# A hybrid decoder layer: loads of the opening in order of use over two queues, and row factors turned on chip before they are stored

## The chip, the cores and the metric

The kernel runs on one core of a Trainium2 chip. The metric is the device time of one execution in microseconds (us). Five engines work beside each other: PE (TensorE, matmuls; its weight loads are PEld), DVE (VectorE), ACT (ScalarE), POOL (GpSimd) and SP (SyncE, which here only issues transfers). Each engine takes its instructions in a fixed order and waits on semaphores. SP, ACT and POOL can issue DMA transfers; sixteen DMA engines carry them out.

## The reference

One inference step of one layer for 4096 prompt tokens and 64 sample tokens (8 sequences of 8), 1024 features each, in float32:

```python
h = x * rsqrt(mean(x * x, axis=-1) + eps) * g_pre      # one factor per token, one gain per feature
z = h @ w_in                                           # 1024 -> 2816 columns, split into
cb, cc, ch, cg, q, k, v, ag, mq, mg = split(z)         # conv, attention and memory groups
u = cc * ch;  conv = conv_w[0]*u[t-2] + conv_w[1]*u[t-1] + conv_w[2]*u[t]
out_a = silu(cg) * cb * conv                           # new conv state: the last two rows of u
out_b = silu(ag) * window_attention(q, k, v, sink)     # 128-wide causal window, one sink per head
out_c = silu(mg) * memory_attention(mq, mk, mv)        # 256 memory tokens
y = concat(out_a, out_b, out_c) @ w_out
x = x + rmsnorm(y) * g_post
```

Outputs are the new x for prompt and sample tokens, the new window keys and values, the convolution's states (two rows of u per sequence; called o_convp for the prompt and o_convs for the eight sample sequences) and the memory's keys and values.

## The kernel before

The 4160 tokens stand as columns, 520 to a block, eight blocks (b = 0 to 7), each of two halves of HW = 260. The in-projection is done in three phases of the weight's columns, 0, 1 and 2, all eight blocks in each. Within a block the product of a 2x2 split of weights (A11, A12, A21, A22) and of inputs (B11 to B22) is made with seven products over sums and differences of the parts (S1 to S4, T1 to T3). Only blocks 0 and 1 of phase 0 are "plain", with eight products of the parts themselves. The name of a buffer tells the part: x_0B is a part B of block 0, w_0A a part A of weight quarter 0, lo_2T the low half of a T of block 2, place a buffer that keeps an input part of a block.

float32 is kept by splitting each operand into hi (a rounded copy) and lo (the rest); `product` (L392) makes hi·hi, lo·hi and hi·lo over four k of 128 features, twelve matmuls of 128x128 by 128x260 to a bank; a product has four banks in phases 0 and 1, thus 48 matmuls, and is called a step here. DVE adds the banks into z (`evict`, L399). In phase 2 the attention runs between the products, and the output projection (L1675) follows.

The order of all engines' work is written out: in each step a list of jobs is put between the matmuls, and each engine's instructions stand in the order in which the program writes them.

**Opening.** SP and ACT issue the loads of the first input part x(0, B11) (in two halves of k, 128x2x260 each, written x_0B) and of the four quarters of the weight part A21 (wr_0A to wr_3A), then of A11. While they fly PE runs idle matmuls (L737). DVE copies w_0A's hi part, ACT makes hi_0B (x times the gain, L613), DVE lo_0B and w_0A's lo part; then the 48 matmuls of the first product begin. In this first step each bank takes hi·hi for all four k, then the lo parts of x, then those of the weights (`product`, opening=True).

**Row factors.** The factor of a token is 1/sqrt of its mean square. Tokens are also loaded as rows (nat, 104 tokens by 1024 features); in phase 0 ACT squares and sums five such tiles per block (`row_step`, L300), POOL turns the sums into factors r (104x5; L315, L316), and

```python
G.dma_start(rowd[b].rearrange("(i p) -> p i", p=RG), r[:RG, 0:5])    # L321
```

stores them as 520 single elements into DRAM (rowd). Some steps later `rows_load` (L284) reads the 520 floats back with SP, spread to all 128 partitions (rb), and `scale` (L363) multiplies them onto the inputs of that block on DVE. What counts the steps is `row_spreads[b] = 4`, taken down by one at the start of each step in `row_queue` (L341), which loads at 1. The blocks 0 and 2 get theirs in another way at first: DVE writes the factors into a diagonal (`rows_diag`, L328), and PE multiplies it with ones.

**Queues.** In phase 0 SP issues the loads (x parts, weights, nat, rb, and ws, the weight parts from which sums are made in `w_sums`, L234) and POOL all stores (L200: th into md, z parts into qd, v into vd, scaled inputs into hd, sums into sd). From phase 1 on the stores go to SP (L202). A load that has to wait holds what SP has behind it.

**Convolution.** In block 0 of phase 1 POOL writes the sample part of u (us), and its last two rows per sequence go out from there with SP as runs of 8 bytes, twice. The prompt's (o_convp) go out at the end of that phase.

## Time and profile before

| what | us |
|---|---|
| three runs: median (lowest to highest) | 1458.19 (1456.69 to 1459.25) |
| the profiled execution's own time | 1455.13 |
| its span in the trace | 1453.4 |
| PE busy | 1442.0 |
| DVE busy | 1206.5 |
| ACT busy | 756.0 |
| POOL busy | 447.1 |

The profile is that of one execution, and its span is what the trace covers of that execution's own time. In timelines each row has the start and the duration in us, the engine, the source line, the operation with out<-in, and in brackets how long the engine stood before it and what released it. Instructions of one line that follow each other are drawn together (x4). In rows of windows the busy time of PE, PEld, DVE, ACT and POOL (with the count of instructions) is followed by the clock that PE was granted, the busy share of the DMA engines and the rate in GB/s. TensorE's granted clock over the whole execution was 0.999. A line behind "x7:" has the shortest, median and longest duration in ns.

### The profile page before, as it was taken

The page shows a single profiled execution, that of the slowest core. Times are in us where ns is not written, and L with a number is a line of the kernel's source. Part 1 is how long each engine was busy: PE and PEld are TensorE (multiplying, and loading weights), DVE is VectorE, ACT ScalarE, POOL GpSimd, SP SyncE. Part 2 cuts the span into 40 slices and gives each one's busy share as a digit, 9 for nine tenths or more (in the row PEclk, how much of TensorE's full clock was granted, in tenths as well). Part 3 has the DMA queues.
Part 4 walks back from the last instruction along what each step waited for, and adds up shares of the span by engine and source line. Part 5 has one row for each costly group of instructions (what it writes and reads, how often), then busy time and mean ns, then how long its engine had stood idle before and what let it go on. Part 6 is the DMA issues. An engine that isn't in the chain of part 4 may idle for free.

```text
span 1453.4 us, 30932 instructions
## 1 busy us (share of the span) xinstructions
PE 1442.0 (99%) x11453; PEld 1324.3 (91%) x11453; DVE 1206.5 (83%) x1899; ACT 756.0 (52%) x1868; POOL 447.1 (31%) x622
## 2 busy tenths in 40 slices
PE   9999999999999999999999999999999999999998
PEld 9999999999999999999999999978777787777777
DVE  6879888899998877799678778998998889888853
ACT  6776665566522222234445534656566555655641
POOL 0223323212300000000002224275665566556661
PEclk9999999999999999999999999999999999999999
DMA  9999999896866644475987978999988899998773
GB/s 266 160 275 232 293 269 277 238 307 215 226 223 198 192 136 150 140 273 143 323 276 228 290 231 266 324 261 238 238 217 224 215 258 228 238 237 223 233 220 105
DMA packets 212124, 337.27 MB, mean 232 GB/s; under 512 B 55301, under 2 KB 126213, under 8 KB 211941
## 3 DMA queue, kind: packets, MB, share of 16 engines
q1 hardware_dynamic: 159189, 226.29, 52.7%
q0 software_dynamic: 44144, 78.68, 21.3%
q10 hardware_dynamic: 8640, 30.33, 6.7%
q8 instruction: 91, 1.49, 0.5%
q14 instruction: 60, 0.49, 0.1%
HBM read 192.48 MB, written 110.15 MB: 208 GB/s over the span
## 4 chain that ended last, share of the span: by engine, by line
PE 82%; DMA 8%; DVE 4%; issue 3%; ACT 2%; SPq 1%; POOL 1%; POOLq 0%; ACTq 0%; DVEq 0%
PE c L397 46%; PE y L1675 24%; PE pv L1144 5%; PE ws L1144 3%; DMA place<-in_xt 2%; PE xs L1144 2%; DMA nat<-in_x_p 2%; DMA wr_3A<-in_w_in 1%; PE mem_acc L825 1%; DMA md<-th 1%; DVE z L649 1%; DMA x_1B<-in_xt 1%; DMA vd<-v 1%; DMA wr_3S<-sd6S 1%; DMA w<-s 0%
## 5 line engine op out<-in xcount | busy, mean ns | idle before, releaser
L1675 PE MATMUL y<-wo,mh 128*128 128x512 f32 (+1 forms) x1040 | 328.7, 391 | 0.0
L403 DVE TENSOR_TENSOR z<-c,z 128x520 f32<-128x520 f32 (+1 forms) x308 | 193.6, 644 | 61.3 <-PE c L397 60.5
L1675 PEld LDWEIGHTS y<-wo,mh 128*128 128x128 f32 x1040 | 194.2, 188 | 52.4 <-DVE wmx L1303 5.4
L1675 PE MATMUL y<-wo,ml 128*128 128x512 f32 (+1 forms) x520 | 201.0, 387 | 0.0
L1347 POOL TENSOR_SCALAR s<-s,x 128x256 f32<-128x256 f32 x124 | 58.0, 480 | 199.1 <-DVE x L1342 193.5
L1675 PEld LDWEIGHTS y<-wo,ml 128*128 128x128 f32 x520 | 97.8, 188 | 18.5
L1313 ACT ACTIVATE s<-s,wnm 128x128 f32<-128x128 f32 x256 | 98.7, 387 | 0.0
L771 POOL MEMSET negs<- 128x1 f32 x1 | 0.1, 100 | 281.7 <-DVE w_2A L219 281.7
L1290 ACT COPY s<-ws 128x256 f32<-128x256 f32 x128 | 41.3, 378 | 77.4 <-PE ws L1144 68.5
L1705 POOL TENSOR_TENSOR xr<-yn,xr 128x1024 f32<-128x1024 f32 x29 | 69.3, 2390 | 18.4 <-ACT yn L1704 17.7
L1378 POOL TENSOR_SCALAR_AFFINE_SELECT wd<-w 128x512 f32<-128x512 f32 x64 | 60.2, 941 | 38.2 <-DMA w<-s 21.7
L1683 ACT ACTIVATE y<-y 128x512 f32<-128x512 f32 (+1 forms) x66 | 38.6, 585 | 52.8 <-DVE yn L1682 52.7
L1336 ACT ACTIVATE s<-xs,x 128x256 f32<-128x256 f32 x128 | 58.1, 461 | 0.0
L1682 DVE TENSOR_TENSOR yn<-y,gpost 128x512 f32<-128x512 f32 (+1 forms) x66 | 44.7, 677 | 16.0 <-PE y L1675 14.5
L1144 PEld LDWEIGHTS ws<-kst,q 64*128 64x128 f32 x768 | 47.7, 185 | 11.0 <-issue 9.5
L1378 POOL TENSOR_SCALAR_AFFINE_SELECT w<-w 128x512 f32<-128x512 f32 x64 | 55.5, 887 | 2.2
L1144 PE MATMUL ws<-kst,q 64*128 64x256 f32 x768 | 55.0, 288 | 0.0
L1294 DVE COPY_PREDICATED s<-wmask,ws 128x256 f32<-128x256 uint8 x124 | 48.0, 441 | 8.0 <-ACT s L1290 6.0
L309 ACT ACTIVATE nat<-nat 104x1024 f32<-104x1024 f32 x40 | 42.3, 1058 | 19.2 <-DMA nat<-in_x_p 19.2
L405 ACT COPY z<-c 128x520 f32<-128x520 f32 (+1 forms) x44 | 24.1, 553 | 53.0 <-PE c L397 50.0
L1313 ACT ACTIVATION_READ_ACCUMULATOR s<-s,wnm 128x1 f32 x256 | 47.9, 187 | 0.0
L200 POOL DMA_DIRECT2D md<-th x48 | 26.2, 547 | 66.9 <-DVE th L457 40.3
(970 smaller groups left out, 4805.6 us busy)
## 6 DMA issues: line engine op xcount, KB each, us to landing
w<-s SPq DMA_DIRECT2D x456, 64.0 KB
q<-qd POOLq DMA_DIRECT2D x32, 768.0 KB, 6.6
xr<-in_x_p SPq DMA_DIRECT2D x32, 512.0 KB
nat<-in_x_p SPq DMA_DIRECT2D x39, 416.0 KB
o_yp<-xr SPq DMA_DIRECT2D x31, 512.0 KB
md<-th POOLq DMA_DIRECT2D x48, 260.0 KB, 7.0
qd<-zh SPq DMA_DIRECT2D x48, 260.0 KB
qd<-z SPq DMA_DIRECT2D x48, 260.0 KB
```

Of the source, the lines that this page charges most:

```text
L309: S.activation(t[:RG], t[:RG], AF.Square, accum_out=r[:RG, i : i + 1])
L397: TE.matmul(bank[:, :HW], w[:, l, k * P : (k + 1) * P], h[r][:, k], start=first and i == 0, stop=last and i == 3 * KH - 1)
L403: add = lambda dst, other: V.tensor_tensor(dst, c, other, op=ALU.add)
L1144: ins = TE.matmul(o, w, x, **kw)
L1294: V.copy_predicated(to, squares(third["wmask"]), squares(s3[:, :, 0:P]))
L1313: S.activation(sm[:, h], sm[:, h], AF.Exp, bias=nm[:, h : h + 1], scale=SCALE, accum_out=den[:, h : h + 1])
L1336: S.activation(p[:, i], s[:, i].rearrange("p (a k j) -> p a k j", a=2, k=4), AF.Exp, bias=nm[:, i : i + 1], scale=SCALE, accum_out=den[:, ...
L1347: G.tensor_scalar(p[:, i], p[:, i], rd[:, i : i + 1], 0.5, op0=ALU.mult, op1=ALU.mult)
L1378: G.affine_select(out, src, pattern=[[32 * sign, 2], [0, 8], [sign, 32]], compare_op=op, fill=0.0, base=base * sign, channel_multiplier=-s ...
L1675: TE.matmul(acc, self.hl[l][:, k], wo[k][c0 // 512][:, r, c0 % 512 : c0 % 512 + c1 - c0], start=j == 0, stop=j == passes * KT - 1)
L1682: V.tensor_tensor(yn[:m, c0:c1], acc[:m], gpost[0][:m, c0:c1], op=ALU.mult)
L1705: total = G.tensor_tensor(self.xr, yn, self.xr, op=ALU.add)
```

## The change

1. *Opening.* POOL writes ones before the identity. The idle matmuls are nine instead of seven, on ones by ones. The second half of x_0B is issued by ACT; the weights all by SP. ACT makes hi k0, w_0A's hi part, hi k1 to k3; DVE follows with lo k0, w_0A's lo part, lo k1 to k3. The first product's matmuls go through k in pairs, with the three kinds for each.
2. *Row factors.* POOL copies r into a zeroed 128x32 tile (turned); two steps later DVE transposes it in place in squares of 32, and POOL stores it with four transfers of 5x32, 5x32, 5x32 and 5x8 elements. Block 0's are stored too (as they were) and not loaded. The load of rb stays at its step.
3. *First diagonal.* `rows_diag` of block 0 goes from the end of step (0, 7) to step (0, 6).
4. *Convolution's state.* POOL copies the two rows to a packed 128x16 tile, stored as 64-byte runs; the two o_convp stores move to step (2, 3, 0).

```diff
-    make_identity(nc, ident)
     ones = const.tile([P, P], F32, name="ones")
     G.memset(ones, 1.0)
+    make_identity(nc, ident)
...
+    turned = const.tile([P, 32], F32, name="turned")
+    G.memset(turned, 0.0)
...
-                DMA.dma_start(t[:, k : k + parts, g - g0 : g - g0 + w], src[:, KH * kh + k : KH * kh + k + parts, off : off + w])
+                queues[k // parts % len(queues)].dma_start(t[:, k : k + parts, g - g0 : g - g0 + w], src[:, KH * kh + k : KH * kh + k + parts, off : off + w])
...
-            G.dma_start(rowd[b].rearrange("(i p) -> p i", p=RG), r[:RG, 0:5])
-            if b > 0:
-                row_spreads[b] = 4
+            G.tensor_copy(turned[:RG, 0:5], r[:RG, 0:5])
+            row_spreads[b] = 4
...
-        for b in [b for b, n in row_spreads.items() if n == 1]:
+        for b in [b for b, n in row_spreads.items() if n == 3]:
+            V.transpose(turned, turned)
+            for g in range(0, RG, 32):
+                n = min(32, RG - g)
+                G.dma_start(rowd[b].rearrange("(i p) -> i p", p=RG)[:, g : g + n], turned[g : g + 5, :n])
+        for b in [b for b, n in row_spreads.items() if n == 1 and b > 0]:
             rows_load(b)
...
-        order = [(l, r, k) for l, r in ((0, 0), (0, 1), (1, 0)) for k in range(KH)] if opening else \
+        order = [(l, r, k + n) for k in (0, 2) for l, r, n in ((0, 0, 0), (0, 1, 0), (0, 0, 1), (1, 0, 0), (0, 1, 1), (1, 0, 1))] if opening else \
...
-            store(a["o_convs"][ct], us[:, :, 8:10])
+            last = tiny.tile([P, 16], F32, tag="x4", name=f"convs{ct}")
+            G.tensor_copy(last.rearrange("p (b t) -> p b t", b=NB), us[:, :, 8:10])
+            store(a["o_convs"][ct].rearrange("p b t -> p (b t)"), last)
...
-            (0, 6): lambda: [*parts(1, "B11"), *row, *fills(1, "S1", "S4"), *sums(3, 0), *row],
-            (0, 7): lambda: [*row, *fills(3, "S2", "S3"), lambda: rows_diag()],
+            (0, 6): lambda: [*parts(1, "B11"), lambda: rows_diag(), *row, *fills(1, "S1", "S4"), *sums(3, 0), *row],
+            (0, 7): lambda: [*row, *fills(3, "S2", "S3")],
...
-    x_of(0, 0, "B11", 2)
-    first_w("A21", 0, queue=S)
+    x_of(0, 0, "B11", 2, (DMA, S))
     S.mul(tiny.tile([P, 16], F32, tag="x4", name="table")[:, :8], mhalf, 1.0)
-    first_w("A21", 1, queue=S)
-    first_w("A21", 2, 3)
+    first_w("A21")
     first_w("A11", 0, 1)
     x_of(0, 0, "B21")
...
-    for _ in range(7):
-        TE.matmul(idle[:, 0, :P], ones, ident, start=True, stop=True)
-    w = ws[0, 0, "A21"] = w_slot(0, "w0_0A21")
-    V.tensor_copy(w[:, 0], raw0[0, "A21"])
-    x_split(0, "B11")
-    V.tensor_tensor(w[:, 1], raw0.pop((0, "A21")), f(w[:, 0]), op=ALU.subtract)
+    for _ in range(9):
+        TE.matmul(idle[:, 0, :P], ones, ones, start=True, stop=True)
+    x_split(0, "B11", 0)
+    first_fill("A21", 0)
+    x_split(0, "B11", 1, 2, 3)
```

The order of ACT at the start of the program, before and after (x_0B is the first input part, wr a weight quarter as loaded, w its split):

```order
L83 DMA gpre<-in_gpre 128x8
L225 DMA wr_0A_217<-in_w_in 128x512
L729 ACT_TABLE_LOAD
L729 ACTIVATE table<-mhalf 128x8
L225 DMA wr_1A_221<-in_w_in 128x512
L613 ACTIVATE hi_0B_243<-x_0B_214,gpre 128x260 x4
L215 CAST w_1A_254<-wr_1A_221 128x512
```

```order
L83 DMA gpre<-in_gpre 128x8
L274 DMA x_0B_216<-in_xt 128x2x260
L737 ACT_TABLE_LOAD
L737 ACTIVATE table<-mhalf 128x8
L622 ACTIVATE hi_0B_245<-x_0B_216,gpre 128x260
L218 CAST w_0A_249<-wr_0A_221 128x512
L622 ACTIVATE hi_0B_245<-x_0B_216,gpre 128x260 x3
L218 CAST w_1A_258<-wr_1A_223 128x512
```

The two weight loads of ACT have gone to SP, one half of the input has come to it, and the cast of w_0A, which was DVE's, stands between the first hi and the other three.

The order of POOL in phase 0 from a block's row factor on (block 3's products run, the factor is the next block's; md, hd, qd are stores), before and after:

```order
L316 TENSOR_TENSOR r_1647<-r_1647,mhalf 104x5
L321 DMA rowd_82<-r_1647 104x5x1
L200 DMA md<-th_2_1948 128x520
L200 DMA md<-th_4_1965 128x520
L200 DMA hd_B_116<-place 128x1040
L200 DMA md<-th_6_2038 128x520
L200 DMA qd<-zh_0_2042 128x520
L200 DMA qd<-kl__2044 128x520
L200 DMA md<-th_3_2062 128x520
L200 DMA md<-th_5_2066 128x520
L200 DMA md<-th_7_2118 128x520
```

```order
L319 TENSOR_TENSOR r_1666<-r_1666,mhalf 104x5
L324 COPY turned<-r_1666 104x5
...
L203 DMA hd_B_118<-place 128x1040
L203 DMA md<-th_6_2057 128x520
L203 DMA qd<-zh_0_2061 128x520
L203 DMA qd<-kl__2063 128x520
L203 DMA md<-th_3_2081 128x520
L203 DMA md<-th_5_2085 128x520
L352 DMA rowd_84<-turned 5x32 x3
L352 DMA rowd_84<-turned 5x8
L203 DMA md<-th_7_2142 128x520
```

A copy stands where the store stood, and the four stores of the factors come eight stores later, behind md of th_5 and ahead of md of th_7.

More of the change, by code (lines that the diff above doesn't have):

```diff
@@ L260, in x_tile, with x_load @@
         return place[:, kept.index(o)] if o in kept else hxp.tile([P, KH, HW], F32, tag="hx", name=f"x{ph}_{b}{o}")
-    def x_load(ph, b, o, parts=KH):
+    def x_load(ph, b, o, parts=KH, queues=(DMA,)):
         kh, g0 = int(o[1]) - 1, (2 * b + int(o[2]) - 1) * HW
@@ L460, in finish_gate @@
         store(md[idx, :, tokens(b)], th)
-    ub_prev, us_of = [None, None], []
+    ub_prev, us_of, convp = [None, None], [], []
     def us_load():
@@ L493, in finish_conv @@
         if b == NBLK - 1:
-            store(a["o_convp"][ct], ub_prev[ct])
+            convp.append(lambda: store(a["o_convp"][ct], ub_prev[ct]))
         acc = temp(f"cacc{b}_{ct}")[:, :n]
@@ L554, in h_split, with x_of @@
             hs[i] = split(xs[ph, b][o], f"{ph}_{b}{o}", (ph, b) == (1, 1) and p < 2)
-    def x_of(ph, b, o, parts=KH):
+    def x_of(ph, b, o, *parts):
         if ph == 0 or b < PLAIN_BLOCKS:
-            t = x_load(ph, b, o, parts)
+            t = x_load(ph, b, o, *parts)
         else:
@@ L606, in hybrid_layer, with x_split @@
     raw0, zz, pending, h0, kept = {}, {}, {}, {}, {}
-    def x_split(b, o):
+    def x_split(b, o, *ks):
         x = xs[0, b][o]
-        h0[b, o] = hi, lo = [h_tile(n, f"{n}0_{b}{o}") for n in ("hi", "lo")]
-        for k in range(KH):
+        hi, lo = h0[b, o] = h0.get((b, o)) or [h_tile(n, f"{n}0_{b}{o}") for n in ("hi", "lo")]
+        for k in ks or range(KH):
             g = gain_of(o, k)
@@ L1024, in input_projection @@
                 jobs.append(us_load)
+            if (ph, b, p) == (2, 3, 0):
+                jobs += convp
             if ph == 1 and NP_ * b + p + 2 in V_TURNS:
```

## The prediction

> **What bounds the kernel now.** I read the page's busy shares first, then the waits of PE, the timeline of the opening, and the stretches in which transfers collapse.
>
> ```profile
> span 1453.4 us, 30932 instructions
> PE 1442.0 (99%) x11453; PEld 1324.3 (91%) x11453; DVE 1206.5 (83%) x1899; ACT 756.0 (52%) x1868; POOL 447.1 (31%) x622
> ```
>
> The matmuls fill 1442.0 of 1453.4 us, so 11.4 us is all that an edit off PE can win by removing idle time, unless PE's own pace changes. The waits of PE (us in total, times, longest) show how little of that stands inside:
>
> ```profile
> PE c L397 <- DVE lo_1T L386: 1.0, 1, 1.0
> PE c L397 <- DVE lo_1B L386: 0.7, 1, 0.7
> PE c L397 <- DVE lo_6B L386: 0.3, 1, 0.3
> PE c L397 <- DVE lo_2T L386: 0.2, 1, 0.2
> ```
>
> Four stalls, 2.2 us in all. Now the opening (start, duration, engine, line, and in brackets the idle time before with what ended it):
>
> ```profile
> 0.80 0.97 SPq L271 DMA_DIRECT2D x_0B<-in_xt  x2
> 1.26 0.45 ACTq L225 DMA_DIRECT2D wr_0A<-in_w_in  x1
> 1.54 3.35 PE L737 MATMUL idle<-ident,ones 128*128 128x128 f32 x14 [1.54 <-POOL mhalf L89]
> 4.01 0.91 ACT L613 ACTIVATE hi_0B<-x_0B,gpre 128x260 fp32r<-128x260 f32 x2 [0.77 <-DMA x_0B<-in_xt]
> 5.20 0.43 DVE L739 CAST w_0A<-wr_0A 128x512 fp32r<-128x512 f32 x1 [5.20 <-DMA wr_0A<-in_w_in]
> 5.54 1.68 DVE L614 SCALAR_TENSOR_TENSOR lo_0B<-x_0B,gpre,hi_0B 128x260 fp32r<-128x260 f32 x4
> 5.76 0.91 ACT L613 ACTIVATE hi_0B<-x_0B,gpre 128x260 fp32r<-128x260 f32 x2 [0.84 <-DMA x_0B<-in_xt]
> 5.77 1.54 PE L397 MATMUL c<-hi_0B,w_0A 128*128 128x260 f32 x4 [0.88 <-DVE w_0A L739]
> 7.75 0.61 ACT L215 CAST w_2A<-wr_2A 128x512 fp32r<-128x512 f32 x1
> 8.91 0.99 PE L397 MATMUL c<-hi_0B,w_1A 128*128 128x260 f32 x4
> 9.74 0.64 PE L397 MATMUL c<-lo_0B,w_1A 128*128 128x260 f32 x4
> 13.53 0.28 PE L397 MATMUL c<-lo_0B,w_0A 128*128 128x260 f32 x1
> ```
>
> The first real matmul starts at 5.77. From 8.91 to 9.74 four matmuls take 0.83 us, 0.207 us each; from 9.74 to 13.53 thirty-two take 3.79 us, 0.118 us each. So the clock is let go at about 9.7, some 3.9 us after the steady work began at 5.77, although 3.35 us of idle passes had run before it with a gap of 0.88 us.
>
> **The opening.** The two halves of x_0B leave SP at 0.80 and about 1.28; the second releases ACT at 5.76. In the change the second half goes to ACT's queue and wr_0A takes its place on SP. Its landing is bounded by its own 5.20 and the 5.76 of the transfer whose place it takes; I take 5.5. The cast is then ACT's (0.61, by the row of w_2A) where it was DVE's (0.43), and with the 0.14 us from cast to matmul that stands here (5.20 + 0.43 to 5.77) the first real matmul comes at 5.5 + 0.61 + 0.14 = 6.25, 0.5 us later than now.
>
> What follows goes faster. ACT does hi k0 from 4.01 to 4.47, the cast to 6.1, then hi k1 to k3 at 0.455 each to 7.5. DVE does w_0A's low part (0.69, by the row of L237 below, of the same shape) to 6.8 and then lo k1 to k3 at 0.42 each to 8.05. The last two of the twelve matmuls hang on lo k3, so the first product can't end before about 8.3 (now 8.91). With a free clock the other thirty-six take 36 x 0.118 = 4.25 us and the four products end at 12.6: 0.95 us ahead of 13.53. With the slow clock until 3.9 us after 6.25, thus 10.15, the first product ends at 6.25 + 12 x 0.207 = 8.75, seven more matmuls go at the slow pace and the rest at the fast one: 10.15 + 29 x 0.118 = 13.6, no gain. Which of the two? The idle run is eighteen passes for fourteen, 18/14 x 3.35 = 4.3 us, and starts about 0.5 us sooner, as it no longer waits for ident and mhalf; unbroken it is longer than the 3.9 us after which the clock came here. I lean to the early release and take two thirds, **-0.65 us**; bounds -0.95 and +0.5 (wr_0A at 5.76 and the clock half a microsecond later than reckoned).
>
> The Trainium skill, "TensorE: Matmul & The Clock Gate", Part 1, says that the gate looks at a free-running window of some 3.4 us, so that the same kernel finds it at another phase in each run. By that rule the 4.3 us need not decide, and the release may come in some runs before 6.25 and in others well after 10; the 3.35 us that released nothing here agree with it (the late clock among the rivals).
>
> Of queues the skill says ("DMA: Bandwidth & Descriptors", Issuing engines are not separate DMA queues) that transfers from several issuing engines share the same sixteen DMA engines and save only issue time. By it the second queue wins nothing here and wr_0A lands at 5.76, a quarter microsecond behind my 5.5; no row of this case shows the new order.
>
> **The row factors.** Seven stores of 520 four-byte elements leave POOL in phase 0 (L321). The second fence has the windows of DMA around one of them: PE, PEld, DVE, ACT, POOL busy, the granted clock, the DMA share and GB/s last.
>
> ```profile
> L321 POOL DMA_DIRECT2D rowd<-r x7: 990/1001/1177, 42.2 to 260.1; - x7
> DMA to landing us min/median/max: 8.7/11.5/14.5
> ```
>
> ```profile
> 220.40 1.00 POOL L321 DMA_DIRECT2D rowd<-r  x1 [0.30 <-POOL r L316]
> ```
>
> ```profile
> 224.00:228.00 4.00, 4.00 (x36) 4.00 (x35) 4.00 (x6) 3.87 (x7) 0.99 (x2) 1.00 0.80 66
> 228.00:232.00 4.00, 4.00 (x36) 4.00 (x36) 3.51 (x4) 0.25 (x2) 1.41 (x4) 1.00 0.90 170
> 232.00:236.00 4.00, 4.00 (x37) 4.00 (x36) 2.37 (x4) 3.99 (x7) 1.36 (x3) 1.00 1.04 389
> ```
>
> The store is followed by 8 us in which 66 and 170 GB/s move while the DMA engines are busy: the small writes hold everything behind them. But PE is busy for all 12 us: here the pause is paid by slack. What it leaves behind is a backlog, and the place where that may reach PE is a load of block 6:
>
> ```profile
> 247.75 13.21 DMA place<-in_xt
> 265.82 0.40 PE L397 MATMUL c<-hi_6B,w_3A 128*128 128x260 f32 x2
> 266.51 0.36 PE L397 MATMUL c<-lo_6B,w_0A 128*128 128x260 f32 x1 [0.30 <-DVE lo_6B L386]
> ```
>
> The chain of waits goes from that load, 13.2 us in flight, over ACT and DVE to lo_6B. Two matmuls need 2 x 0.118 of the 0.69 us from 265.82 to 266.51, so 0.45 us are lost. Runs of 128 bytes make some seventeen pieces of 520; the pause should go with the pieces. I take the whole **-0.45 us**; bounds 0 (the load is late from ordinary traffic, since the pause ended 15 us earlier) and -0.85 (the stall at lo_2T goes as well: 0.63 us for two matmuls there, 0.4 lost; its chain shows DVE work and no transfer, so I leave it):
>
> ```profile
> 117.59 0.40 PE L397 MATMUL c<-hi_2T,w_3S 128*128 128x260 f32 x2
> 118.22 0.36 PE L397 MATMUL c<-lo_2T,w_0S 128*128 128x260 f32 x1 [0.23 <-DVE lo_2T L386]
> ```
>
> What is added: per block a POOL copy, four POOL issues and a DVE transpose. The rows are that of a larger transpose and, for the last edit, one from the chain of waits of phase 1.
>
> ```profile
> L894 DVE STREAM_TRANSPOSE vq<-vl x8: 700/704/706, 430.4 to 589.5; 128x512 f32<-128x512 f32 x8
> 368.30 7.54 DMA x_1B<-in_xt
> ```
>
> A 128x32 transpose is a sixteenth of 128x512: between 0.05 and, if a fixed cost dominates, 0.2 us; I take 0.1. Six of the seven fall where PE doesn't wait for DVE; block 3's row factor is stored two steps after 105 and its transpose lands in the DVE chain ahead of lo_2T: **+0.1 us** (0 to 0.4, should it meet two stalls). POOL's four issues at 0.54 us (md's row below) replace one of 1.0, 1.2 us more per block, and with the copy under 2 us; POOL is busy 31%, and this lies under its waits for DVE. The earlier diagonal of block 0 moves five small DVE operations one step forward, inside a step whose PE work doesn't wait: 0. If that cover failed, they would cost their own time, under 1.5 us. The convolution's state goes out in 128 pieces instead of 1024, twice, and the two last stores go to a later phase: 0; the stalls near it, lo_1B and lo_1T, hang on a load of x_1B that leaves at 368.3 and flies 7.5 us, and on DVE work behind it.
>
> **Sum.** -0.65 - 0.45 + 0.1 = -1.0. The profiled execution took 1455.13 us, 1.7 around its span of 1453.4; it would take 1454.1. The runs' median is 1458.19, 3.1 above it, and moves by the same amount: **1457.2 us**.
>
> **Rivals.** *The row load's wait takes the place of what was won* (slower). The store now goes out two steps of 48 x 0.118 = 5.7 us later, on POOL behind md_5, and the load that reads it back stays where it was; on SP this load stands ahead of the next block's weights. In block 5 (the last two rows: who waited for the weights' loads, and the issues' table of the page):
>
> ```profile
> 192.35 0.54 POOL L200 DMA_DIRECT2D md<-th  x1 [0.75 <-DMA rowd<-r]
> 195.20 0.34 SPq L284 DMA_DIRECT2D rb<-rowd  x1
> 195.65 2.79 SPq L234 DMA_DIRECT2D ws2A<-in_w_in  x4
> 204.59 0.69 DVE L237 TENSOR_TENSOR ws2S<-ws2A,ws2A 128x512 f32<-128x512 f32 x1
> 207.17 1.24 DVE L386 TENSOR_TENSOR lo_4B<-place,hi_4B 128x1040 fp32r<-128x1040 f32 x1
> 209.24 0.28 PE L397 MATMUL c<-lo_4B,w_0S 128*128 128x260 f32 x1
>   DVE ws2A L238: 0.7, 1
> md<-th POOLq DMA_DIRECT2D x48, 260.0 KB, 7.0
> ```
>
> The four stores follow the md store of 192.35 and the last leaves at about 195.1. Should it land as POOL's large stores do (the last row: 7.0 us in the median), SP stands until 202.1, and ws2A leaves at 202.4, 6.8 us later than now. DVE takes it at 204.59, has waited 0.7 us for it already, and lo_4B ends at 208.41, 0.83 us before PE wants it. If the loads flew as long as now, PE would lose 6.8 - 0.8 = 6 us; if the queue has emptied meanwhile, the 1 MB at the 389 GB/s of the window above is in by 205.1 and the slack holds. Between them, nearer the low end, 1.5 us in each of the four blocks that load sums (4 to 7): +6 - 1 = +5, **1463.2**. It decides from a landing about 7 us after the last issue with an empty queue, and sooner with a full one. Against it: those 7.0 us were measured with the pause in front, which is to go.
>
> *The small writes cost more than I see* (faster). The stores of the convolution's state make a pause too:
>
> ```profile
> 392.00:396.00 4.00, 4.00 (x36) 4.00 (x35) 4.00 (x8) 0.78 (x1) 3.71 (x5) 1.00 0.48 21
> ```
>
> If it also drives the two stalls of phase 1, 1.7 us by the waits, and lo_2T's 0.4 and the full 0.95 come in: -0.95 - 0.45 - 0.4 - 1.7 = -3.5, **1454.7**. Against it: DVE is busy for the whole of that window (4.00), and the chain has no transfer after x_1B's.
>
> *The change doesn't do what it says*: the clock stays slow until 10.15 and the late load of block 6 has other causes: 0 to +0.5, **1458.4**.
>
> *The late clock*: the steady work needs as much again as the idle run that released nothing, 3.35 us beyond 10.15. Each microsecond at the slow pace loses 1 - 0.118/0.207 = 0.43, so +1.4, less 0.35 for the other two terms, **1459.3**. This is what the free-running window of the skill's page would give in a run of bad phase.
>
> **How the numbers follow.** The forecast has 0.45, the row load's wait 0.18, the larger gain 0.17, no effect 0.12, the late clock 0.08. What the runs can tell from no change is 0.2%, 2.9 us. Faster by more: most of the larger gain and a little of the forecast, 0.22. Slower: the row load's wait, 0.17. Same: 0.61. The forecast's own bounds are -1.8 (all three terms at their best, -0.95 - 0.85) to +0.9 (+0.5 + 0 + 0.4), 1456.4 to 1459.1; with the rivals, and the 1.5 us by which single runs stray from the median, the range is 1453.6 to 1461.4, which leaves most of the slow case out.
>
> **What would show it.** Right: the first real matmul near 6.25 and the first matmul on A11 near 12.6 to 13; no window under 200 GB/s in the 12 us after a row store; place<-in_xt of block 6 under 10 us and no wait at lo_6B; SP's row load issued within 5 us of the last row store and no wait of DVE for ws2A beyond the 0.7. Wrong: an idle time of PE near lo_3B to lo_6B at the weights' sums, a pace of 0.207 beyond 10.2, or a new wait at lo_1B that is not there now.

## The result: 0.8% slower

| kernel | median us | lowest to highest | runs |
|---|---|---|---|
| before, on the same chip | 1457.44 | 1455.25 to 1459.25 | 6 |
| changed | 1469.05 | 1467.33 to 1470.17 | 6 |

The ratio is 1.0079, with a 95% interval from 1.0069 to 1.0090: slower by 11.6 us. It lies outside the range forecast. The profiled execution took 1470.17 us with a span of 1468.5, 15.1 us more than the span of before: the profiled execution of before, 1455.13, lay 2.3 us under its median, that of the changed kernel 1.1 above.

The head of the page and the waits of PE in the changed kernel (in us: in total, times, longest):

```profile
span 1468.5 us, 30982 instructions
PE 1449.2 (99%) x11457; PEld 1330.8 (91%) x11457; DVE 1210.5 (82%) x1905; ACT 758.4 (52%) x1869; POOL 460.9 (31%) x653
```

```profile
PE ws L1152 <- DMA q<-qd: 7.0, 1, 7.0
PE pv L1152 <- ACT y L1691: 2.3, 5, 1.2
PE c L404 <- ACT w_0A L218: 1.2, 1, 1.2
...
PE c L404 <- DVE lo_1T L393: 0.8, 1, 0.8
```

lo_2T and lo_6B, the two stalls in the terms of the sum, are gone, and so is lo_1B at the start of phase 1. But a wait of 7.0 us stands first that was not there before, for a load of queries in the attention of phase 2, 700 us behind the last edit of the row factors. And PE is busy 7.2 us longer than before with four more matmuls: it also runs slower somewhere.

Setting the same matmul of both programs side by side, by its start, gives the course of the loss (changed minus before, in us):

| place, us of the trace before | 20 | 105 | 125 | 255 | 275 | 380 | 405 | 680 | 950 | 980 | 1025 | 1185 | 1365 | 1445 |
|---|---|---|---|---|---|---|---|---|---|---|---|---|---|---|
| behind by | 1.0 | 1.4 | 0.8 | 1.7 | 1.3 | 1.7 | 0.6 | 1.8 | 2.1 | 12.0 | 12.4 | 13.6 | 15.2 | 15.1 |

An opening that loses 1.0 us where it was to win 0.65. Three gains where stalls went: 0.6 between 105 and 125 (lo_2T), 0.4 at 265 (lo_6B), 1.0 between 380 and 405 (lo_1B and part of lo_1T). Around them a steady drift, as in the 1.1 us from 405 to 640, where neither kernel has a stall. And ten microseconds in one place near 975. The 2.7 us from 1025 on come in small steps in the output projection's part of the program; in the traces of the twelve kernels below the same stretch gives -0.3 to +2.4 us against before's trace, so I take this piece as what single executions stray by.

**The place of the ten microseconds.** First PE around the stall, then POOL and SP, which issue the transfers ahead of it (timelines: start, duration, and in brackets the idle time before and what ended it; q is a load of queries from qd, place a load of stored parts from md):

```profile
974.70 0.38 PE L1152 MATMUL ws<-kst,q 64*128 64x256 f32 x2
982.10 2.72 PE L1152 MATMUL ws<-kst,q 64*128 64x256 f32 x22 [7.02 <-DMA q<-qd]
```

```profile
962.42 3.99 POOL L1370 DMA_DIRECT2D w<-s  x8 [0.77 <-DVE s L1302]
...
968.29 0.90 POOL L1190 DMA_DIRECT2D q<-qd  x1 [1.28 <-issue]
```

```profile
961.90 5.15 SPq L1370 DMA_DIRECT2D w<-s  x8
...
967.86 0.51 SPq L1198 DMA_DIRECT2D place<-md  x1
```

The load q (768 KB) leaves POOL at 968.29, 0.43 us *behind* the load place (1024 KB) that SP issues at 967.86. It is 13.8 us in flight, and PE needs it at 975. In the kernel before the same two are the other way round:

```profile
964.87 0.89 POOL L1182 DMA_DIRECT2D q<-qd  x1
```

```profile
965.79 0.45 SPq L1190 DMA_DIRECT2D place<-md  x1
```

There q leaves 0.92 us *ahead* of place. The landings of all such loads, before and changed, in us (shortest, median, longest):

```profile
DMA to landing us min/median/max: 5.9/6.6/11.1
```

```profile
DMA to landing us min/median/max: 5.5/6.8/13.8
```

This one is the 5.9 of before and the 13.8 of the changed kernel. What made POOL late is in its row: it stood 1.28 us, and nothing that the profile shows released it ("issue"). Its eight loads of w began 0.52 us behind SP's eight, as in the kernel before (960.33 and 959.82), so POOL was not late until then. The stall then costs a second time, through the clock (windows: busy PE, PEld, DVE, ACT, POOL, granted clock, DMA share, GB/s; before, then changed):

```profile
980.00:1000.00 20.00, 20.00 (x136) 16.06 (x135) 17.59 (x35) 13.72 (x57) 9.84 (x12) 1.00 0.84 211
```

```profile
980.00:1000.00 20.00, 17.90 (x112) 14.91 (x113) 13.73 (x24) 9.80 (x35) 9.47 (x12) 0.80 0.71 185
```

A mean clock of 0.80 over these 20 us is 8 us at half speed. The clock records of the trace put the half-speed stretch at 977.8 to 988.1, 10.24 us, which is three stretches of 3.41 us, begun while PE stood. Only what lies behind the stand costs anything: from 982.1 to 988.1 PE does 6.0 us at half speed, 3.0 us more. 7.0 + 3.0 = 10.0, against 9.9 to 10.3 by the table.

### The profile page after: what moved, and what is told of

Same layout as the page of the kernel before. It is cut to its first block, busy times and chain, and to the rows that moved or that the text cites. A ratio compares the mean times of both kernels' runs of the same rounds, so it can differ in the third digit from the quotient of the medians.

```text
span 1468.5 us, 30982 instructions
## 1 busy us (share of the span) xinstructions
PE 1449.2 (99%) x11457; PEld 1330.8 (91%) x11457; DVE 1210.5 (82%) x1905; ACT 758.4 (52%) x1869; POOL 460.9 (31%) x653
## 4 chain that ended last, share of the span: by engine, by line
PE 83%; DMA 5%; issue 4%; SPq 3%; DVE 3%; POOL 1%; ACT 1%; ACTq 0%; POOLq 0%; DVEq 0%
PE c L404 54%; PE y L1683 20%; PE pv L1152 4%; SPq L1370 2%; PE ws L1152 2%; DMA o_yp<-xr 1%; DMA q<-qd 1%; PE xs L1152 1%; DMA w<-s 1%; PE mem_acc L831 1%; DMA place<-md 1%; DMA vd<-v 0%; DMA x_1B<-in_xt 0%; DMA wr_1S<-sd2S 0%; POOL md L203 0%
## 5 line engine op out<-in xcount | busy, mean ns | idle before, releaser
L1690 DVE TENSOR_TENSOR yn<-y,gpost 128x512 f32<-128x512 f32 (+1 forms) x66 | 44.7, 678 | 13.7 <-PE y L1683 12.4
L1712 ACT ACTIVATE yn<-yn,yst 128x1024 f32<-128x1024 f32 x29 | 33.4, 1152 | 21.6 <-POOL yst L1704 21.6
L1337 DVE TENSOR_REDUCE x<-xs 128x2 f32<-128x512 f32 x64 | 43.7, 683 | 0.0
```

Source lines behind the costliest of these rows:

```text
L1337: V.tensor_reduce(mx, s, axis=AX.X, op=ALU.max)
L1690: V.tensor_tensor(yn[:m, c0:c1], acc[:m], gpost[0][:m, c0:c1], op=ALU.mult)
```

## The experiments

The kernels were timed in three groups of four, each with the kernel before beside it: its median was 1461.18 us (31 runs) in the first group, 1460.04 (13) in the second and 1460.57 (29) in the third. So kernels of different groups are compared by their ratios to it. Where no ratio is given there was one timed run.

### Which half: the opening alone, and the rest alone

*Opening alone*, the first item of the change on the kernel before:

```diff
+    x_of(0, 0, "B11", 2, (DMA, S))
+    first_w("A21")
...
+    for _ in range(9):
+        TE.matmul(idle[:, 0, :P], ones, ones, start=True, stop=True)
+    x_split(0, "B11", 0)
+    first_fill("A21", 0)
+    x_split(0, "B11", 1, 2, 3)
...
```

> The kernel before with the opening of the change alone; the row factors, the first diagonal and the convolution's stores are as before. The profile of the change showed two things: the opening about 1 us later (the clock comes at 5.0, falls back to half from 8.4 to 11.8), and a load of q on POOL's queue near 968 us that was issued 1.3 us late and cost PE 7 us of standing and 10 us at half clock. Theory 'count': POOL's issue stands whenever the running count of pieces of all its transfers passes a multiple of some 960 per DMA engine; the row factors' stores moved that place from mix<-md (929) to q (968). The opening leaves POOL's count alone, so this kernel shows only the opening: +0.5 to +1.5 us. Theory 'lateness': everything behind a late start meets its partners at another time, and the q load loses its place for that reason; then the opening alone, which is 1 of the 2 us of lateness, may bring the stand too: +8 to +12 us.

Measured: 1461.46, ratio 1.0001 (0.9988 to 1.0015). The opening neither wins nor loses anything measurable. POOL's q is on time, and no wait for q stands in this trace.

*All but the opening*, the other three items alone (the edit is against the changed kernel):

```diff
-    x_of(0, 0, "B11", 2, (DMA, S))
+    x_of(0, 0, "B11", 2)
+    first_w("A21", 0, queue=S)
...
-    for _ in range(9):
+    for _ in range(7):
...
```

> The change without its opening: row factors turned and stored in runs, first diagonal a step sooner, convolution's stores packed and moved; the opening is that of before. 'Count': POOL's running count at the q load is the same as in the change, so the stand of about 7 us and the half clock come here too: +8 to +11 us, less some 1.5 to 2 us won at lo_2T, lo_6B and the start of phase 1: +7 to +10 against before. 'Lateness': the start is on time, no stand at q: -1.5 to -2 us.

Measured: 1465.47, ratio 1.0033 (1.0020 to 1.0047), and the stall is here:

```profile
PE ws L1155 <- DMA q<-qd: 4.7, 1, 4.7
```

```profile
969.19 0.90 POOL L1193 DMA_DIRECT2D q<-qd  x1 [1.28 <-issue]
```

Again 1.28 us of unexplained standing, again behind place (968.75), then 4.7 us of wait and a clock of 0.86 over 980 to 1000. The row factors bring the stall, and a loss of 4.8 us by the ratio, less than the 7 to 10 expected. With the opening, which alone costs nothing, it is 11.5 us in the whole change. Part of the difference is the stall itself, 10.0 us there and 7.2 here (4.7, and 2.5 through a half-speed stretch of 6.83 us); why it is longer with the same 0.43 us between place and q, and where the rest of the difference lies, isn't settled.

### Why POOL stands: a stand that moves from load to load

A stand is here an idle time of POOL ahead of a transfer that nothing in the profile ends. The kernel before has one too, 39 us earlier and at a load that nobody waits for:

```profile
929.11 0.90 POOL L1190 DMA_DIRECT2D mix<-md  x1 [3.82 <-issue]
```

In the changed kernel that load goes out without such a stand, and the stand is at q. What differs on POOL between the two is the number of pieces (runs of bytes that lie together) its transfers have had by then: seven row stores of 520 pieces went, twenty-eight of 5 pieces came. I counted for each POOL transfer its pieces over 16, rounded up, plus one (a rule fitted to the traces): a row store is 34 before, and four stores are 8 now, so 7 x (34 - 8) = 182 fewer are counted by then. In both kernels the stand is at the transfer that carries this sum past about the same value (1885 to 1950 at mix; 1882 to 1931 at q). If that is right, putting some 200 back must send the stand back to mix, and with it end the stall.

*The change with pieces put back*: eight stores of 384 pieces of 128 bytes to a place that nobody reads, at 680 to 690 us, eight by 25 = 200:

```diff
+    FILL = {(0, 4): 2, (0, 5): 2, (0, 6): 2, (1, 0): 2}
...
+    def filler():
+        t = tc.dram_tile([3, P, 32], F32, name=f"fill{len(fillers)}")
...
+        G.dma_start(t.rearrange("k p n -> p k n"), ones[:, : 3 * 32].rearrange("p (k n) -> p k n", k=3))
...
+            if ph == 2 and (b, p) in FILL:
+                jobs += [filler] * FILL[b, p]
```

> The whole change, and eight small stores by POOL of a constant to scratch memory (384 pieces of 128 bytes each, 25 places per DMA engine, 200 in all) at about 680 to 690 us, where POOL has nothing to do; eight, so that each later transfer keeps its semaphore. They leave no trace in any output. 'Count': the multiple of 960 now falls on mix<-md at about 930 us, as in before, and the stand of PE at 975 is gone: 10 us faster than the change, about +1 against before. 'Lateness': the timing of everything else is that of the change, and the stand stays: +11 us against before.

Measured: 1460.62, ratio 0.9996 (0.9982 to 1.0009), from the 1.0079 of the change without them. By the two ratios, eight useless stores take some 12 us off (0.0083 x 1460). The stand is at mix, q leaves 0.85 us ahead of place (969.40 and 970.25), and no wait for q is left:

```profile
932.95 0.89 POOL L1208 DMA_DIRECT2D mix<-md  x1 [3.57 <-issue]
```

*The kernel before with more pieces*, sixteen stores of 768 pieces of 64 bytes (16 by 49 = 784 in the count above), meant to bring the stand to q there:

```diff
+    FILL = {(0, 4): 4, (0, 5): 4, (0, 6): 4, (1, 0): 4}
...
+        t = tc.dram_tile([6, P, 16], F32, name=f"fill{len(fillers)}")
...
```

> The kernel before, and sixteen small stores by POOL to scratch memory (768 pieces of 64 bytes each, 49 places per DMA engine, 784 in all) at about 680 to 700 us. Nothing else is changed. 'Count': the third multiple of 960, 2880, now falls on the q load at 965 us (2848 to 2897), and the kernel before gets the stand of the change: +8 to +11 us. 'Lateness': the timing of before is kept, no stand: within 1 us of before.

Measured: 1462.52, ratio 0.9998 (0.9986 to 1.0010): a miss. The stand at mix went, for the sum now passes that value at a filler (692.6, without a stand there). But none came to q at 968; a short one, 0.92 us, is at a q of 1139.89. Either pieces of 64 bytes count otherwise, or the sum can't be carried on so far.

*The kernel before with a small, like-sized addition*: the same eight stores from the first 64 partitions, 192 pieces of 128 bytes each, 8 by 13 = 104:

```diff
+        G.dma_start(t.rearrange("k p n -> p k n")[:64], ones[:64, : 3 * 32].rearrange("p (k n) -> p k n", k=3))
```

> The kernel before with eight smaller fillers by POOL (192 pieces of 128 bytes, 13 places each, 104 in all) at 680 to 690 us. Theory 'count': the stand of POOL that is at mix<-md (3.8 us, places 1886 to 1950) moves to a transfer some 104 places sooner, to the q load of about 924 us (then 1891 to 1940). Theory 'place in the program': it stays at mix<-md. The sixteen fillers of 64 bytes did not move it to the q load at 968; this one tells whether that was the count or the form of those pieces.

Measured: 1460.44 beside 1460.57 for before. The stand left mix for the load ahead of it, an earlier q, as the sum says (1891 to 1940):

```profile
927.88 1.68 POOL L1192 DMA_DIRECT2D q<-qd  x2 [2.15 <-issue]
929.55 0.91 POOL L1200 DMA_DIRECT2D mix<-md  x1
```

So the stand followed the count of pieces from the kernel before to the changed one, back to mix with 200 added, and to the earlier q with 104 added; it did not follow the 784. Only this one value fits: the changed kernel has a second stand, 0.62 us at a q of 1245 (2868 to 2917), and the kernel before passes the same count at 1170.8 without one. Why POOL stands when the sum passes such a value, no row shows.

### What the stand costs: the order against the large load

If the loss comes from q's place behind the 1 MB load and not from the stand itself, moving that load back must cure most of it with the stand left as it is.

```diff
-            at(0, 0, lambda: chunks[2].load_mix())
+            at(0, 2, lambda: chunks[2].load_mix())
```

> The change, with the 1 MB load place<-md of chunk 2 two transfers later on SP's queue; POOL's order and count are as in the change. POOL still issues the q load 1.3 us late. Theory 'lost place in the queue': the q load flies 12 to 14 us only because the 1 MB load is issued 0.4 us ahead of it; now it is behind, q lands within 6 to 8 us, PE's stand is under 2 us, and the kernel is about 8 us faster than the change. Theory 'late issue is enough': q still lands over 10 us after its issue and PE stands 5 us or more.

Measured, the changed kernel with this alone: 1464.38 in one run, beside 1460.04 for before. POOL and SP:

```profile
969.92 0.90 POOL L1190 DMA_DIRECT2D q<-qd  x1 [1.30 <-issue]
```

```profile
969.39 0.46 SPq L1638 DMA_DIRECT2D xr<-in_x_p  x1
970.30 0.34 SPq L1720 DMA_DIRECT2D o_yp<-xr  x1
970.68 0.43 SPq L1198 DMA_DIRECT2D place<-md  x1
```

```profile
PE ws L1152 <- DMA q<-qd: 2.9, 1, 2.9
```

The stand is the same 1.3 us, q leaves ahead of place and flies 9.7 us instead of 13.8; PE waits 2.9 us instead of 7.0, and the clock stays at 1.00 over 980 to 1000. This lies between the two theories. The lost place in the order was the larger part, 4.1 of the 7.0 us of wait; xr still goes ahead of q.

### The drift: 128 bytes per partition

The new tile turned, 128x32 floats, is 128 bytes per partition and stands ahead of all later buffers. *The kernel before with the tile alone, never read*:

```diff
+    turned = const.tile([P, 32], F32, name="turned")
+    G.memset(turned, 0.0)
```

> The kernel before, and one unused tile of 128x32 in the pool of constants, zeroed once by POOL, at the place where the change has `turned`. It moves every later buffer of SBUF by 128 bytes and does nothing else. In the traces so far the matmuls of phase 1 follow each other at 118.33 ns in the three kernels without this tile and at 118.89 ns in the three with it. Theory 'place in memory': 118.89 ns here too, some 2.5 to 3 us more over the 5400 matmuls of phases 0 and 1. Theory 'traffic' (the new stores, copies and transposes slow PE's reads): 118.33 ns, no difference.

The total of the one run, 1459.56, is too coarse for this. The pace isn't: over 200 us in which PE never stands, the count of matmuls is (before, changed, before with the tile):

```profile
430.00:630.00 200.00, 200.00 (x1692) 200.00 (x1691) 165.92 (x234) 48.53 (x55) 0.00 (x0) 1.00 0.52 166
```

```profile
430.00:630.00 200.00, 200.00 (x1684) 200.00 (x1684) 165.19 (x232) 48.85 (x56) 0.00 (x0) 1.00 0.52 162
```

```profile
430.00:630.00 200.00, 200.00 (x1685) 200.00 (x1684) 165.09 (x233) 48.72 (x56) 0.00 (x0) 1.00 0.51 163
```

At the same clock, 1692 matmuls against 1684 and 1685. The mean from one matmul to the next in this window is 118.33 ns before and 118.89 in both kernels with the tile. The tile, and with it the move of all later buffers by 128 bytes, is shown to be enough. The starts of the same matmuls say it over all traces. From 405 to 640, where none has a stall, the five traces with the tile (changed, this one, all but the opening, pieces put back, late place) each fall 1.1 us behind before; the eight without it stay within 0.02. From 100 to 275 the four of these five that have the new row stores lose 1.2 us against the five that have the new stores and no such tile. With 0.3 us from 20 to 100 and 0.4 from 275 to 375 the tile costs about 3.0 us. Most of it sits in few places: in the window above, 105 of the 1681 steps from one matmul to the next take 124 to 127 ns with the tile (105 or 106 in each of the five traces), where none of the nine traces without it has one over 121. All of them follow a matmul on weight quarter 0 or 3 (w_0, w_3), none one on 1 or 2. So certain buffers are slower at their new place; why, no row tells.

### The versions that keep the gain

*The change without the opening, turned laid into a free row of zs (an existing tile), pieces put back as above*:

```diff
-    turned = const.tile([P, 32], F32, name="turned")
+    turned = zs[:, 10, :32]
```

> The change without its opening, with `turned` put into a part of a tile that is there anyway and is not used in phase 0 (a row of zs), so that no buffer moves, and with the eight filler stores of before, so that POOL's stand falls on mix<-md. If place in memory, POOL's count and the opening explain all that the change loses, this one has the gains of its row factors alone: no stalls at lo_2T and lo_6B, a pace of 118.33 ns, no wait of PE for q: 1 to 2 us faster than before. If one of them is wrong: the pace stays at 118.89 (same as before, within 1 us) or PE stands for q (+5 us and more).

Measured: 1457.22, ratio 0.9985 (0.9969 to 1.0000). The pace is back, 1692 matmuls in the window, and q leaves ahead of place again:

```profile
430.00:630.00 200.00, 200.00 (x1692) 200.00 (x1691) 166.02 (x233) 48.53 (x55) 0.00 (x0) 1.00 0.52 164
```

```profile
964.10 0.90 POOL L1202 DMA_DIRECT2D q<-qd  x1
```

```profile
964.99 0.44 SPq L1210 DMA_DIRECT2D place<-md  x1
```

*The whole change with the same two repairs and twelve idle matmuls*:

```diff
-    turned = const.tile([P, 32], F32, name="turned")
+    turned = zs[:, 10, :32]
...
-    for _ in range(9):
+    for _ in range(12):
```

> As the last kernel, but with the change's opening, and twelve idle matmuls instead of nine. In the change the idle passes end at 5.2 us, the first real matmul comes at 6.4, and the clock, let go at 5.0, falls back to half for 3.4 us at 8.4. Theory 'gap': the pause of 1.2 us lets the clock fall back; with twelve, PE has work until about 6 to 6.6, the clock stays, and the first four products end at 12.6 to 13.2 instead of 14.5. Theory 'phase': the clock is looked at in fixed stretches of 3.4 us that begin at another moment in each run, and the end may lie anywhere from 12.6 to 15.6, as it does for kernels with the same opening (13.5 and 14.2 for that of before, 14.3 to 15.6 for that of the change).

Measured: 1468.21 in one run, a miss that taught the most. The stall is back without a stand at q:

```profile
960.51 1.53 POOL L1395 TENSOR_SCALAR_AFFINE_SELECT wd<-w 128x512 f32<-128x512 f32 x2 [5.91 <-DMA w<-s]
962.10 1.40 POOL L1395 TENSOR_SCALAR_AFFINE_SELECT w<-w 128x512 f32<-128x512 f32 x2
963.46 3.99 POOL L1379 DMA_DIRECT2D w<-s  x8
...
968.02 0.90 POOL L1199 DMA_DIRECT2D q<-qd  x1
```

```profile
961.99 4.95 SPq L1379 DMA_DIRECT2D w<-s  x8
...
967.61 0.54 SPq L1207 DMA_DIRECT2D place<-md  x1
```

```profile
PE ws L1161 <- DMA q<-qd: 5.2, 1, 5.2
```

This time POOL's eight loads begin 1.47 us behind SP's: it had waited 5.9 us for earlier loads of w, and its work on them ended late. q left 0.41 us behind place, PE waited 5.2 us, and the clock records show half speed from 980.7 to 987.6. A wait of 1.57 us for ACT at 733.49, the first piece of this trace's loss, was followed by half speed too, from 734.97 to 738.39. In the opening the clock came at 4.52 and stayed, and the four first products ended at 13.0, as the theory of the gap has it and within what that of the phase allows. So the stand is one way to lose the place among others; the lead of 0.92 us in the kernel before is what was thin.

*The repaired rows with the large load moved back too* (the first kernel of this section with the edit of the order):

```diff
-            at(0, 0, lambda: chunks[2].load_mix())
+            at(0, 2, lambda: chunks[2].load_mix())
```

> The row factors of the change with `turned` in a row of zs and the eight fillers (the version that was about 2 us faster than before), and place<-md of chunk 2 behind the next two transfers of SP, so that the q load can't lose its place to it. The fast runs should stay where that version was; runs in which POOL comes late for any reason lose less. Expected 0.997 to 0.999 of before; if the 1 MB load is now late for its own use at the group behind, 1 us slower than that version.

Measured: 1457.56 beside 1460.57, ratio 0.9975 (0.9964 to 0.9986), 3.0 us less by the medians. It beats both kernels; no wait for q stands in its trace. By the starts of the same matmuls the row stores account for 1.25 us of it against before's trace, and for 0.5 to 3.1 against other traces with the old stores (worked out below).

*The same without the eight stores*:

```diff
-            if ph == 2 and (b, p) in FILL:
-                jobs += [filler] * FILL[b, p]
...
```

> The same without the fillers: POOL's stand falls on the q load again (1.3 us), but the 1 MB load is behind it. If the stand costs PE much only because it loses q's place in the queue: within 2 us of the last kernel, a wait of PE for q under 3 us. If 1.3 us late is enough by itself: PE stands 5 us or more and the kernel is at 1.003 of before, as the row factors alone were.

Measured: 1460.70, ratio 0.9996 (0.9985 to 1.0007).

```profile
965.16 0.90 POOL L1192 DMA_DIRECT2D q<-qd  x1 [0.45 <-issue]
```

```profile
PE ws L1154 <- DMA q<-qd: 1.8, 1, 1.8
```

q leaves behind xr (964.52) and flies 9.5 us; the 3 us are lost again, though the clock stays at 1.00 over 980 to 1000. That is neither theory: the wait is under 3 us as in the first, but the kernel is 3.1 us above the last one. Nor does this trace isolate the stand, 0.45 us here: POOL's eight loads of w already began 1.38 us behind SP's (960.11 and 958.73), as in the miss above. Issuing q from another queue or a step sooner, which would need no useless stores, wasn't tried.

*The best version with the change's opening and twelve idle matmuls*:

```diff
+    x_of(0, 0, "B11", 2, (DMA, S))
...
+    for _ in range(12):
```

> The first kernel of this call with the opening of the change and twelve idle matmuls. In the one look before, the clock came at 4.5 and stayed, and the four first products ended at 13.0 instead of 13.5 to 14.2 (opening of before) and 13.2 to 15.6 (that of the change with nine). If twelve hold the clock in every run: 0.5 to 1 us faster than the first kernel of this call. If the phase of the clock decides: the same, within 1 us.

Measured: 1458.58, ratio 0.9986 (0.9974 to 0.9999), not better than 0.9975 without that opening. In its trace the first step ends 0.5 us sooner than before's, but 1.9 us are lost again by 66 us, at two short waits of PE (w_0A at 25, lo_0B at 31) and beside them; in the kernel above with the same twelve matmuls nothing is lost there. The opening's half microsecond is below what these runs can tell. POOL's loads of w began late here too, 1.18 us behind SP's; with place moved back, q left at 968.02, 1.76 us ahead of it, flew 7.6 us, and PE did not wait for it.

## Why the prediction was wrong

**The failing step is the costing of POOL's issues in "What is added".** They were priced at under 2 us a block, and "this lies under its waits for DVE". At their own place that is right. What was missed is that POOL's later issues depend on how many pieces went before: the change takes 182 counted pieces away, a stand of POOL moves from mix, where it cost nothing, to q, and q falls behind a megabyte. That is ten of the 15.1 us between the traces, and about all of the 11.6 between the medians by the kernel with pieces put back. The trace of before held both warnings, unread: the row of mix with its 3.82 us of "issue", and the 0.92 us by which q led place. I asked of every edit what hides it, but only at the place of the edit.

**The row load's wait, the slower rival, had the right kind of mechanism and the wrong load.** It did not occur. The last row stores of a block and the load that reads them back:

```profile
231.29 2.08 POOL L352 DMA_DIRECT2D rowd<-turned  x4
```

```profile
237.37 0.36 SPq L287 DMA_DIRECT2D rb<-rowd  x1
237.82 1.80 SPq L237 DMA_DIRECT2D ws4A<-in_w_in  x4
```

The last store landed at 237.24, and SP's load went out at 237.37, 4.0 us after the last issue at 233.4; its point of decision was 7 us. No wait of PE or DVE for ws followed.

**The pause: right in kind, mis-sized.** The new stores and the window after one:

```profile
L352 POOL DMA_DIRECT2D rowd<-turned x28: 521/527/751, 47.1 to 272.7; - x28
DMA to landing us min/median/max: 3.6/5.0/7.9
```

```profile
232.00:236.00 4.00, 4.00 (x35) 4.00 (x34) 3.46 (x6) 2.12 (x3) 2.50 (x5) 1.00 0.94 283
236.00:240.00 4.00, 4.00 (x36) 4.00 (x35) 2.39 (x4) 0.53 (x1) 0.00 (x0) 1.00 0.49 139
240.00:244.00 4.00, 4.00 (x36) 4.00 (x36) 2.06 (x3) 1.59 (x3) 0.00 (x0) 1.00 0.98 317
```

They land in 5.0 us where it took 11.5; the collapse to 66 GB/s is gone (the 139 comes with DMA engines busy half the time, so little was asked). The block-6 load of place flies 6.1 us instead of 13.2, and lo_6B no longer waits. The issues cost what was reckoned, 0.527 us each against 0.54; a block's factors are 20 pieces (four stores of 5) and not some seventeen, and the transpose takes 0.21 us where 0.1 was taken. What it brings can be read from all traces, by the start of the same matmuls from 100 to 275, against before's trace: +0.6, +0.2 and +1.9 us in three others with the old stores and the old place in memory (their stalls are at lo_4T, lo_4T, and lo_3B to lo_5T), and -1.25 in each of the five with the new stores and the old place in memory, where PE waits for DVE nowhere in that stretch. With the tile, the one trace with the old stores has no such wait either and loses 0.5 us against the four with the new ones. So the old stores' stalls wander from trace to trace and cost between 0.5 and 3.1 us; none is left in the nine traces with the new stores. The term of -0.45, with -0.85 as its bound, was too small: I read two stalls of one execution as the whole, and left lo_2T out because its chain shows no transfer.

**The stores of the convolution's state: 0, and the traces show no more,** though the changed kernel's own trace seems to say otherwise: between 380 and 405 its lag falls by 1.0 us, lo_1B's stall is gone and lo_1T's went from 1.0 to 0.8. The same edit stands in eight other traces, and there that stretch gives -1.2 to +0.9 us; in the four without it, -0.6 to +0.2. The stall at lo_1T is in all of them, 0.8 to 1.0. One trace would have made this the rival of the small writes.

**The tile was not costed at all.** The part on what is added names the copy and the transpose and not the memory under them: 3.0 us, as worked out above.

**The opening: the term was -0.65, the trace shows +1.0, and the runs of it alone show 0 within 0.15%.** The first real matmul came at 6.43 (6.25 forecast): wr_0A released the cast at 5.76, the other value that the prediction names, and not at 5.5. The clock then went its own way (before, then changed; windows as above. The counts of matmuls give the pace; the column of the clock reads 1.00 ahead of its first change even where the pace is half, as in the first row):

```profile
8.00:10.00 2.00, 2.00 (x12) 2.00 (x12) 2.00 (x4) 1.95 (x4) 0.00 (x0) 1.00 1.05 379
10.00:12.00 2.00, 2.00 (x20) 2.00 (x19) 0.98 (x2) 0.47 (x2) 0.00 (x0) 1.00 1.08 386
```

```profile
8.00:10.00 2.00, 2.00 (x12) 2.00 (x11) 2.00 (x4) 2.00 (x5) 0.00 (x0) 0.61 1.04 372
10.00:12.00 2.00, 2.00 (x11) 2.00 (x11) 1.32 (x3) 0.45 (x2) 0.00 (x0) 0.54 1.08 385
12.00:14.00 2.00, 2.00 (x19) 2.00 (x18) 1.56 (x3) 1.95 (x5) 0.00 (x0) 1.00 1.05 370
```

By the clock's records it came early in the changed kernel, at 5.02, as I leaned to, fell back to half at 8.44 and returned at 11.85: eleven matmuls in the window where before did twenty. "Unbroken it is longer than the 3.9 us after which the clock came here. I lean to the early release" is the step of this term that failed: the release came early and did not stay. Nor was this the change's doing: with the opening of before the clock came at 9.2 to 10.7 in five traces, and at 4.4 to 4.9 in three others, where it also fell back 3.41 us later. The 3.9 us were a fact of one execution. PE's wait of 1.2 us for w_0A lies between the idle run and the work. The same opening began the second product at 14.54 (changed), 14.34, 15.64 and 13.24 in four kernels; the old one lay between 13.35 and 14.28 in eight; twelve idle matmuls gave 13.03 and 13.01 in two, with no fall. By these records the clock changes at multiples of 3.41 us from a start that differs from run to run. The Trainium skill says the same of a free-running window ("TensorE: Matmul & The Clock Gate", Part 1), and it was the better guide here than my count of idle passes. What in a stretch decides that the clock falls is open: one trace of the same opening, that of the second product at 13.24, was released at 5.59 and kept its clock.

**The forecast's other zeros.** The earlier diagonal brought no wait. The forecast of no measurable change, with 0.61, stood on a sum that had terms for phase 0 alone. The range's ends are not sums of the working either: the lowest rival less 1.5 us is 1453.2 and not 1453.6, and 1461.4 is a choice between the forecast and the slow rival.

**The pieces together**, for the two profiled executions: opening +1.0, tile +3.0, row stores -1.25, the stretch at the start of phase 1 -1.0, q and the clock behind it +10.3, the small steps after 1025 +2.7: 14.75 of 15.1.

## What to carry to other kernels

Before an issuing engine's transfers are changed in number or in pieces, go down the rest of its timeline for rows that stand with "issue" as releaser, and for loads that lead a larger one on another queue by less than a microsecond: an edit can be paid for hundreds of microseconds later, on a load it never touches. A wait of PE can cost again at half clock, so a thin lead ahead of a late load is worth widening by the program's order, not by luck. A new constant tile is an edit to every buffer allocated behind it: lay small ones into free rows, and compare matmul counts of a window in which PE never stands.

## What the runs showed of the hardware

- A transfer of 768 KB took 5.9 us when issued 0.92 us ahead of one of 1 MB on another queue, and 13.8 us when issued 0.43 us behind it.
- POOL stands 0.45 to 3.8 us at one transfer between 925 and 970 us of the program, released by nothing in the profile, and which transfer it is moved with the number of pieces issued earlier, where these were of 128 bytes or more; sixteen stores of 64-byte pieces did not fit the count.
- The granted clock fell to half during a wait of PE or within 1.5 us behind it, for whole stretches of 3.41 us: 10.24 us with a wait of 7.0, 6.83 with waits of 4.7 and 5.2, 3.41 with one of 1.6; waits of 2.9 and 1.8 us went with none.
- With all later buffers moved by 128 bytes per partition a matmul takes 118.89 ns in the mean instead of 118.33 at the same granted clock, mostly through 105 of 1681 that take 124 to 127 ns.
- One execution's stalls are not the kernel's: with the old row stores they lay at lo_2T and lo_6B, at lo_4T, from lo_3B to lo_5T, or nowhere in different traces, and cost between 0.5 and 3.1 us against the new ones.
